# A front in a fixed order: loads on two queues, squares of x ahead of those of memory, x's products in place

## The chip, the cores and the metric

The kernel runs on one core of a Trainium2 chip. Its engines work side by side, each through its own queue in order: TensorE (PE, matrix products, with its weight loads listed as PEld), VectorE (DVE), ScalarE (ACT), GpSimd (POOL) and SyncE (SP, which here only issues DMAs). DMAs can be issued by SP, ACT and POOL. The metric is the device time of one execution in microseconds.

## The reference

One layer of a hybrid encoder over 512 frames of 1024 channels in float32, with 256 memory tokens:

```python
u = rmsnorm(h, g_mix[l])
proj = u @ w_in[l]
(gq, gk, gv, gg, ga, fq, fk, fv, ff, mq, gates) = split_cols(proj, PROJ_SIZES)
...
mkv = rmsnorm(mem, g_mem[l]) @ w_mem_kv[l]
mk, mv = jnp.split(mkv, 2, axis=-1)
...
merged = gt[:, :, 0] * y_gla + gt[:, :, 1] * y_fox + gt[:, :, 2] * y_mem
h = h + merged @ w_out[l]
u2 = rmsnorm(h, g_ffn[l])
h = h + jnp.square(jax.nn.relu(u2 @ w_ff1[l])) @ w_ff2[l]
```

Here `rmsnorm(x, g)` is `x * rsqrt(mean(x * x) + 1e-6) * g` over the channels. Three branches (gated linear attention, forgetting attention "FoX", cross attention to the memory) are merged, and an MLP and a last RMSNorm follow. The change touches only the start: the two norms, and the products of the normed memory and the normed x with the first weights.

## The kernel before

**Precision.** Each product of two float32 matrices is made as three products of fp32r parts. A matrix is split into hi (a cast to fp32r on ACT) and lo (the subtract raw - hi on DVE); `mm3` (L149) issues hi x hi, lo x hi and hi x lo into one PSUM tile. So every weight chunk of 128 x 1024 costs a DMA, a cast on ACT and a subtract on DVE, and the same holds for u, the normed x.

**Chunks.** `chunk_list` puts the weights in the order of use. Chunks 0 to 3 are the four key heads of the memory (`w_mem_kv`), 4 to 7 its values, 8 is "G" (low-rank and forget columns, split into the tile `both`), 9 is fq, 10 is fk (the first FoX pair), and 11 to 14 are fv. `load_w`, `split_w` and `get_w` (L132 to L147) load and split a chunk. Raw, hi and lo tiles have three buffers each, so a load waits until an earlier chunk has been split. `gT` and `gN` are generators that issue the products of one chunk or of four; one `next` is one step of three products (a `yield` each).

**The order.** PE runs in the order of the program (`manual_schedule`). On ACT, DVE, POOL and SP a scheduler writes the order ahead of time from its own estimate of the times: of what is ready it takes what was traced first, so later work can fill a gap. `tc.issue_after(ins)` puts what is traced in its block, on the engine of `ins`, behind `ins`.

**The front (L267 to L374).** Twelve products of zeros run first on PE while the first data are loaded. All loads are issued by SP: the columns, then mem (`memr`) in four quarters that alternate with four quarters of chunk 0, then chunk 1, constants, chunk 2, and x (`xr`, with channels on the partitions) in four quarters between chunks 3 and 4. Then:

- mem times `g_mem` is cast to `mxh` on ACT and its rest `mxl` is made on DVE (L301, L302). The norm's factor is applied later, to the products.
- `sq_cols` (L204) squares column block k on ACT and adds it to an accumulator. All sums of mem run on POOL; of x, blocks 1 to 3 on POOL and the others on DVE, in two accumulators.
- `mk_proj(h)` (L336) makes the keys of head h of the memory on PE, evacuates them on ACT, and squares two blocks of x.
- `rms_cols` (L216) sums an accumulator over the partitions by products with a column of ones; `rsqrt` makes the factor on DVE and POOL; `bcast_rows` (L232) spreads it over the partitions: one diagonal on ACT and one product on PE for each 128 frames, then a copy on ACT, to `rmb` (mem) and `rxb` (x).
- `mv` makes the memory's values, 16 steps, evacuated with mem's factor (L344).
- The loop of L359 makes u block by block: product x * `g_mix` * `rxb` on DVE into one of three scratch tiles `sg` (L371), cast to `uhi` on ACT, rest to `ulo` on DVE (L201, L202). For blocks 2 and 5 ACT scales x by `g_mix` beforehand and POOL makes the product (L369). Chunks G and fq are split at block 3.

**Behind it.** `low_rank` (L400) and fq go through PE block by block, five products for each block of u. `mem_split` (L376) scales and splits the memory's keys and values; it stands under `issue_after(u_end)`, where `u_end` is the last `ulo` on DVE. Then come fk (`run(pair)`), `decay_logs` (L418, whose first product is L421) and the four chunks of fv.

Of the kernel before, what the change touches and what calls it, by code (L numbers as in the profile page):

```python
# [3 lines left out]

# [57 lines left out]
def hybrid_block(ctx, tc, chunks, wst, xT, memT, xN, cols, gffn, gfin, wup, cst, out):  # L62
# [25 lines left out]
    def f(ap):  # L88
        return ap.bitcast(F32)
# [107 lines left out]
    def of(hi, lo):  # L197
        return lambda k, sl: (hi[:, k, sl], lo[:, k, sl])
# [2 lines left out]
        nc.scalar.copy(hi, src)  # L201
        return nc.vector.tensor_tensor(lo, src, f(hi), op=ALU.subtract).ins  # L202

    def sq_cols(pool_, src, n, k, accs, pool_ks, tag):  # L204

        e = 1 if k in pool_ks else 0
        eng = nc.gpsimd if e else nc.vector
        if accs[e] is None:
            accs[e] = dct[:, e * S:e * S + S] if n == S else pool_.tile([P, n], F32, tag=f"{tag}_acc{e}", name=nm("acc"))
            nc.scalar.activation(accs[e], src[:, k, :], AF.Square)  # L210
        else:
            sq = pool_.tile([P, n], F32, tag=f"{tag}_sq{e}", name=nm("sq"), bufs=2)
            nc.scalar.activation(sq, src[:, k, :], AF.Square)
            eng.tensor_tensor(accs[e], accs[e], sq, op=ALU.add)

    def rms_cols(pool_, accs, n):  # L216

        accs = [a for a in accs if a is not None]
        ps = at_()
        for t in range(n // P):  # L220
            for i, a in enumerate(accs):
                nc.tensor.matmul(ps[:, t:t + 1], a[:, t * P:(t + 1) * P], ones[:, 0:1], start=i == 0, stop=i == len(accs) - 1)
        return rsqrt(pool_, ps[:, :n // P], 1.0 / D, n // P)

    def rsqrt(pool_, ss, inv, n):
# [6 lines left out]
    def bcast_rows(pool_, r, n, rb):  # L232

        ps = at_()
        for t in range(n // P):
            dg = pool_.tile([P, P], F32, tag="dg", name=nm("dg"), bufs=4)
            nc.scalar.mul(dg, ident, r[:, t:t + 1])
            nc.tensor.matmul(ps[:, t * P:(t + 1) * P], ones, dg, start=True, stop=True)
        nc.scalar.copy(rb, ps[:, :n])
# [27 lines left out]
    with pool("front") as fp:  # L267
        rmb = la[:, 0, :]
        rxb = sg[3]
        memr = fp.tile([P, KT, M], F32, name="memr")  # L270
        xr = fp.tile([P, KT, S], F32, name="xr")
        pre = {}

        def lead(key, n, i):
            if key not in pre:
                late = index[key] > 2
                pre[key] = [(fp if late else wp).tile([P, 1024], F32, tag="lead" if late else "raw", name=nm("raw"),
                                                      bufs=2 if late else 3)]
                pre[key] += [wp.tile([P, 1024], F32R, tag=g, name=nm(g)) for g in ("hi", "lo")]
            sl = slice(i * 1024 // n, (i + 1) * 1024 // n)  # L280
            raw, hi, lo = (t[:, sl] for t in pre[key])
            nc.sync.dma_start(raw, wst[index[key]][:, sl])
            nc.scalar.copy(hi, raw)
            nc.vector.tensor_tensor(lo, raw, f(hi), op=ALU.subtract)
# [10 lines left out]
        nc.scalar.activation(warm, warm, AF.Exp)  # L295
        nc.sync.dma_start(cols_s, cols)
        macc, xacc = [None, None], [None, None]
        for j in range(4):
            nc.sync.dma_start(memr[:, 2 * j:2 * j + 2], memT[:, 2 * j:2 * j + 2])
            for k in (2 * j, 2 * j + 1):  # L300
                nc.scalar.mul(mxh[:, k, :], memr[:, k, :], gmem[:, k:k + 1])  # L301
                nc.vector.scalar_tensor_tensor(mxl[:, k, :], memr[:, k, :], gmem[:, k:k + 1], f(mxh[:, k, :]),  # L302
                                               op0=ALU.mult, op1=ALU.subtract)
                if k == 2 * j:
                    lead(chunks[0], 4, j)
        lead(chunks[1], 1, 0)
        nc.sync.dma_start(cst_s[:, :2 * P], cst[:, :2 * P])
        nc.sync.dma_start(cst_s[:, 5 * P:], cst[:, 5 * P:])
        lead(chunks[2], 1, 0)
        for j in range(4):  # L310
            nc.sync.dma_start(xr[:, 2 * j:2 * j + 2], xT[:, 2 * j:2 * j + 2])
            if j == 1:
                lead(chunks[3], 1, 0)
        lead(chunks[4], 1, 0)
        nc.sync.dma_start(cst_s[:, 2 * P:5 * P], cst[:, 2 * P:5 * P])
        nc.sync.dma_start(wup_s, wup)
        for k in range(KT):
            sq_cols(fp, memr, M, k, macc, range(KT), "m")

        get_plain = get_w  # L320

        def get_first(key):
            return pre[key][1:] if key in pre else get_plain(key)

        get_w = get_first
        UP = (2, 5)

        def mk_evac(h):
            raw = mk_raw(h)
            nc.vector.tensor_tensor(raw, raw, rmb, op=ALU.mult)  # L330
            split(mkh[:, h, :], mkl[:, h, :], raw)

        def mk_raw(h):
            return gkT[h // 2][:, (h % 2) * M:(h % 2) * M + M]

        def mk_proj(h):  # L336
            run(gT(("T", "w_mem_kv", P * h), mxh, mxl, lambda ps: nc.scalar.copy(mk_raw(h), ps[:, :M]), n=M))
            for k in (2 * h, 2 * h + 1):
                sq_cols(fp, xr, S, k, xacc, (1, 2, 3), "x")
                if k in UP:  # L340
                    nc.scalar.mul(xr[:, k, :], xr[:, k, :], gmix[:, k:k + 1])
# [4 lines left out]
        mk_proj(0)
        mk_proj(1)
        rm = rms_cols(fp, macc, M)
        mk_proj(2)
        bcast_rows(fp, rm, M, rmb)  # L350
        mk_proj(3)
        rx = rms_cols(fp, xacc, S)
        nc.vector.tensor_copy(msk_s, cst_s[:, 5 * P:5 * P + 64])
        mv = gN([("N", "w_mem_kv", 2 * j, 512) for j in range(4)], of(mxh, mxl), 2, mmt, mv_evac)
        for _ in range(4):
            next(mv)
        bcast_rows(fp, rx, S, rxb)
        run(islice(mv, 9))
        for k in range(KT):  # L359
            if k == 3:  # L360
                raw = load_w(("G",))
                raw3, w3 = (t.rearrange("p (k c) -> p k c", k=KT) for t in (raw, both))
                nc.scalar.copy(both, raw)
                low = slice(64, P)
                nc.vector.tensor_tensor(w3[:, :, low], raw3[:, :, low], f(w3[:, :, low]), op=ALU.subtract)
                first_q = get_w(("T", "w_in", OFF["fq"]))
            ut = sg[k % 3]
            if k in UP:
                nc.gpsimd.tensor_tensor(ut, xr[:, k, :], rxb, op=ALU.mult)  # L369
            else:  # L370
                nc.vector.scalar_tensor_tensor(ut, xr[:, k, :], gmix[:, k:k + 1], rxb, op0=ALU.mult, op1=ALU.mult)  # L371
            u_end = split(uhi[:, k, :], ulo[:, k, :], ut)
        run(mv)
# [23 lines left out]
    with pool("fox") as xp:  # L397
# [162 lines left out]
        pair = fox_pair(0)  # L560
        for _ in low_rank():
            next(pair)
        with tc.issue_after(u_end):
            mem_split()
        run(pair)
        decay_logs()
        fv = v_chunks(OFF["fv"], v_evac)
        run(islice(fv, 14))
        decay_sums()
# [855 lines left out]
```

## Time and profile before

| what | value |
|---|---|
| median of 3 runs | 816.14 us (815.4 to 816.98) |
| the profiled execution's own time | 815.97 us |
| its span | 814.2 us |
| granted PE clock over the span | 0.994 of full |
| DMA, whole program | 160.75 MB, mean 197 GB/s |
| to 55.5 us: busy PE / DVE / ACT / POOL | 49.50 / 39.30 / 39.38 / 17.35 us |

The profile is one execution. A row of the timeline has a start and a duration in us, engine, line, operation, output and inputs by the program's names, the shape, a count, and in brackets the engine's idle time before it and what ended that. The span of a PE product contains the time in which it passes through the array, so successive products overlap: their price is the distance of the starts. Issue rows of DMAs (SPq, ACTq, POOLq) show the issuing, not the transfer. A window's row has its bounds, its length, the busy time of PE, PEld, DVE, ACT and POOL with the number of instructions, the granted clock, the share of time the DMA engines worked, and GB/s.

### The profile page before, as it was taken

To read this page: it belongs to the slowest core of one execution; us is meant where nothing else is said; L and a number is where in the kernel's file an instruction comes from. 1 tells how busy PE (TensorE), PEld (TensorE's weight loads), DVE (VectorE), ACT (ScalarE), POOL (GpSimd) and SP (SyncE) were. 2 spreads that over 40 slices of the span, in tenths; PEclk is the share of its full clock that TensorE was granted. 3 is DMA by queue.
4 is the path that set the end of the run, shared out by engine and by line. 5 is a ranking of instruction groups with operands and counts; after the bars stand their busy time and mean duration, and the time that the engine had idled before them with its cause. 6 is when DMAs were issued, how large, how long until landed. Compare 5 with 4: busy or idle time off the path is not lost.

```text
span 814.2 us, 12094 instructions
## 1 busy us (share of the span) xinstructions
PE 797.0 (98%) x4625; PEld 681.2 (84%) x4625; DVE 575.6 (71%) x875; ACT 458.2 (56%) x726; POOL 117.5 (14%) x134
## 2 busy tenths in 40 slices
PE   7999999999999999999999999999999999999994
PEld 5878887778888888888888889988998899889983
DVE  5772654454565488585969658885788678878886
ACT  8763554443554346464645546764676377547764
POOL 5201322000000033111110000011001000100131
PEclk9999999999999999999999999999999999999998
DMA  8534968777858768789873706889658956895684
GB/s 313 204 104 138 284 206 225 214 226 208 260 156 224 242 180 183 184 207 234 213 187 113 279 7 225 224 197 221 212 167 196 260 186 164 192 262 186 146 140 129
DMA packets 41034, 160.75 MB, mean 197 GB/s; under 512 B 4952, under 2 KB 6032, under 8 KB 38928
## 3 DMA queue, kind: packets, MB, share of 16 engines
q0 software_dynamic: 11488, 60.30, 35.9%
q1 hardware_dynamic: 27648, 94.93, 33.4%
q10 hardware_dynamic: 1840, 4.75, 1.7%
q8 instruction: 36, 0.59, 0.3%
q14 instruction: 22, 0.18, 0.1%
HBM read 156.26 MB, written 31.49 MB: 231 GB/s over the span
## 4 chain that ended last, share of the span: by engine, by line
PE 93%; DVE 2%; ACT 1%; issue 1%; DMA 1%; POOL 1%; SPq 0%; ACTq 0%; DVEq 0%; POOLq 0%
PE mm L150 20%; PE mm L152 20%; PE mm L151 20%; PE a L150 4%; PE a L151 4%; PE a L152 4%; PE mm L923 3%; PE mm L924 3%; PE mm L925 3%; PE a L924 2%; PE a L923 2%; PE a L925 2%; PE a L547 1%; DMA raw<-in_wst_dram 1%; PE a L503 1%
## 5 line engine op out<-in xcount | busy, mean ns | idle before, releaser
L201 ACT CAST hi<-raw 128x1024 fp32r<-128x1024 f32 x77 | 80.8, 1050 | 62.8 <-PE mm L151 34.3
L202 DVE TENSOR_TENSOR lo<-raw,hi 128x1024 fp32r<-128x1024 f32 x77 | 94.1, 1222 | 30.4 <-ACT hi L201 30.4
L142 DVE TENSOR_TENSOR wlo<-raw,whi 128x1024 fp32r<-128x1024 f32 x49 | 63.0, 1288 | 67.2 <-ACT whi L141 58.7
L141 ACT CAST whi<-raw 128x1024 fp32r<-128x1024 f32 x49 | 51.5, 1052 | 90.6 <-issue 31.5
L1232 POOL DMA_DIRECT2D Y<-in_wst_dram x32 | 27.3, 854 | 263.0 <-DVE lo L202 194.5
L201 ACT CAST hi<-Y 128x1024 fp32r<-128x1024 f32 x40 | 41.9, 1048 | 39.8 <-PE mm L152 29.3
L152 PE MATMUL mm<-u2h,lo 128*128 128x256 f32 x224 | 63.4, 283 | 0.0
L151 PE MATMUL mm<-u2l,hi 128*128 128x256 f32 x224 | 63.4, 283 | 0.0
L150 PE MATMUL mm<-u2h,hi 128*128 128x256 f32 x224 | 63.4, 283 | 0.0
L202 DVE TENSOR_TENSOR lo<-Y,hi 128x1024 fp32r<-128x1024 f32 x40 | 48.9, 1222 | 19.7 <-ACT hi L201 19.6
L151 PE MATMUL mm<-lo,ch 128*128 128x512 f32 x160 | 62.3, 389 | 0.0
L150 PE MATMUL mm<-hi,ch 128*128 128x512 f32 x160 | 62.3, 389 | 0.0
L152 PE MATMUL mm<-hi,cl 128*128 128x512 f32 x160 | 62.2, 389 | 0.0
L150 PE MATMUL mm<-uhi,whi 128*128 128x512 f32 x128 | 50.7, 396 | 0.0
L152 PE MATMUL mm<-uhi,wlo 128*128 128x512 f32 x128 | 49.9, 390 | 0.0
L151 PE MATMUL mm<-ulo,whi 128*128 128x512 f32 x128 | 49.8, 389 | 0.0
L201 ACT CAST hi<-g 128x1024 fp32r<-128x1024 f32 x30 | 31.6, 1054 | 30.4 <-PE a L925 12.3
L202 DVE TENSOR_TENSOR lo<-g,hi 128x1024 fp32r<-128x1024 f32 x30 | 36.6, 1220 | 16.7 <-ACT hi L201 16.6
L150 PE MATMUL mm<-u2sh,hi 128*128 128x256 f32 x168 | 47.5, 283 | 0.0
L151 PE MATMUL mm<-u2sl,hi 128*128 128x256 f32 x168 | 47.5, 283 | 0.0
L152 PE MATMUL mm<-u2sh,lo 128*128 128x256 f32 x168 | 47.5, 283 | 0.0
L151 PEld LDWEIGHTS mm<-u2l,hi 128*128 128x128 f32 x224 | 43.0, 192 | 0.2
(415 smaller groups left out, 2261.0 us busy)
## 6 DMA issues: line engine op xcount, KB each, us to landing
raw<-in_wst_dram SPq DMA_DIRECT2D x109, 512.0 KB, 5.3
Y<-in_wst_dram POOLq DMA_DIRECT2D x32, 512.0 KB, 5.5
raw<-T SPq DMA_DIRECT2D x28, 512.0 KB, 3.4
T<-in_wst_dram POOLq DMA_DIRECT2D x12, 1024.0 KB, 8.9
g<-in_wst_dram POOLq DMA_DIRECT2D x24, 512.0 KB, 5.8
Y<-in_wst_dram SPq DMA_DIRECT2D x16, 512.0 KB, 4.4
g<-in_wst_dram SPq DMA_DIRECT2D x12, 512.0 KB, 3.2
nFb<-dF ACTq DMA_DIRECT2D x8, 448.0 KB, 11.0
```

What stands on the lines that cost most here:

```text
L141: cast = nc.scalar.copy(hi, raw)
L142: nc.vector.tensor_tensor(lo, raw, f(hi), op=ALU.subtract)
L150: nc.tensor.matmul(ps, lh, rh, start=start, stop=False)
L151: nc.tensor.matmul(ps, lh, rl, start=False, stop=False)
L152: nc.tensor.matmul(ps, ll, rh, start=False, stop=stop)
L201: nc.scalar.copy(hi, src)
L202: return nc.vector.tensor_tensor(lo, src, f(hi), op=ALU.subtract).ins
L503: nc.tensor.matmul(pss[e][:, :w], q[half[e], sl], k[half[e], :w], start=a == 0, stop=a == 2)
L923: nc.tensor.matmul(ps[t], a, wh[:, kk, :], start=go, stop=False, **w)
L924: nc.tensor.matmul(ps[t], a, wl[:, kk, :], start=False, stop=False, **w)
L925: nc.tensor.matmul(ps[t], b, wh[:, kk, :], start=False, stop=k == 3, **w)
L1232: nc.gpsimd.dma_start(to, x, accum_op=ALU.add)
```

## The change

The front is rewritten. The new `in_order` chains all ACT, DVE and PE instructions traced in its block: each gets an edge (issue order only) to the one traced before it on the same engine.

- ACT issues the columns and the four quarters of chunk 0, and SP issues mem, then chunk 1, a quarter of x, chunk 2, a quarter, chunk 3, two quarters, two constants, chunk 4. The other constants and `wup` follow behind the squares of mem.
- mem's products and the split of chunk 0 run first, then the splits of chunks 1 and 2, then the keys with the squares of x between the heads. `rms_cols` of x stands in the middle of head 3.
- Squares of mem come later: three ahead of the values, five behind the broadcast of x's factor. All sums are made on DVE, with one accumulator each for x and mem.
- `rms_cols` of mem and its broadcast stand at blocks 0 and 2 of the loop over u.
- x's products are made in place in `xr`, all on DVE; POOL makes none, and ACT no longer scales blocks 2 and 5.
- `mem_split`, fk and `decay_logs` all stand under `issue_after` of the last cast and of the last `ulo`. The mask's copy to `msk_s` moves there.

```diff
+    def in_order():
+        traced = nc.cur_bb.bb.instructions
+        n, mark = len(traced), traced[-1]
+        yield
+        start = next(k for k in reversed(range(len(traced))) if traced[k] is mark) + 1
+        ends = {}
+        for i in traced[start:]:
+            if i.engine in (nc.scalar.engine, nc.vector.engine, nc.tensor.engine):
+                if i.engine in ends:
+                    tc.add_manual_dep(i, ends[i.engine].name,
+                                      mybir.DependencyInfo(mybir.DependencyClass.NoSync, mybir.DependencyReason.DATA),
+                                      reason="in_order")
+                ends[i.engine] = i
+
+    def sq_col(pool_, src, n, k, acc, tag):
+        if k == 0:
+            nc.scalar.activation(acc, src[:, 0, :], AF.Square)
...
+            nc.scalar.activation(sq, src[:, k, :], AF.Square)
+            nc.vector.tensor_tensor(acc, acc, sq, op=ALU.add)
...
+        def first_load(i, n=1):
...
+                (nc.scalar if n > 1 else nc.sync).dma_start(raws[i][:, sl], wst[index[FIRST_W[i]]][:, sl])
...
+        def first_split(i, n=1, j=0):
...
+            cast = nc.scalar.copy(ready[i][0][:, sl], raws[i][:, sl])
+            nc.vector.tensor_tensor(ready[i][1][:, sl], raws[i][:, sl], f(ready[i][0][:, sl]), op=ALU.subtract)
...
+        def first_w(i):
+            run(first_load(i))
+            first_split(i)
...
+        with in_order():
+            nc.scalar.dma_start(cols_s, cols)
+            quarters = first_load(0, 4)
+            for j in range(4):
+                nc.sync.dma_start(memr[:, 2 * j:2 * j + 2], memT[:, 2 * j:2 * j + 2])
+                next(quarters)
+            nc.scalar.activation(warm, warm, AF.Exp)
+            run(first_load(1))
+            nc.sync.dma_start(xr[:, 0:2], xT[:, 0:2])
+            run(first_load(2))
...
+            for k in range(KT):
+                nc.scalar.mul(mxh[:, k, :], memr[:, k, :], gmem[:, k:k + 1])
+                nc.vector.scalar_tensor_tensor(mxl[:, k, :], memr[:, k, :], gmem[:, k:k + 1], f(mxh[:, k, :]),
+                                               op0=ALU.mult, op1=ALU.subtract)
+                if k % 2 == 0:
+                    first_split(0, 4, k // 2)
+            first_split(1)
+            first_split(2)
+            run(mk_proj(0))
+            x_squares(0, 1, 2, 3)
+            first_split(3)
+            run(mk_proj(1))
+            x_squares(4, 5)
+            run(mk_proj(2))
+            x_squares(6, 7)
+            first_split(4)
+            mk3 = mk_proj(3)
+            run(islice(mk3, 4))
+            rx = rms_cols(fp, xacc, S)
+            run(mk3)
+            first_w(5)
+            for k in range(3):
+                sq_col(fp, memr, M, k, macc, "m")
+            mv = gN([("N", "w_mem_kv", 2 * j, 512) for j in range(4)], of(mxh, mxl), 2, mmt, mv_evac)
+            run(islice(mv, 5))
+            bcast_rows(fp, rx, S, rxb)
+            for k in range(3, KT):
+                sq_col(fp, memr, M, k, macc, "m")
+            nc.sync.dma_start(cst_s[:, 2 * P:5 * P], cst[:, 2 * P:5 * P])
+            nc.sync.dma_start(wup_s, wup)
+            for k in range(KT):
+                if k == 0:
+                    first_w(6)
+                    run(islice(mv, 4))
+                    rm = rms_cols(fp, macc, M)
+                if k == 2:
+                    first_w(7)
+                    bcast_rows(fp, rm, M, rmb)
+                    run(islice(mv, 4))
+                if k == 3:
...
+                    nc.scalar.copy(both, raw)
+                    low = slice(64, P)
+                    nc.vector.tensor_tensor(w3[:, :, low], raw3[:, :, low], f(w3[:, :, low]), op=ALU.subtract)
+                    first_w(9)
+                    first_q = ready[9]
+                ut = xr[:, k, :]
+                nc.vector.scalar_tensor_tensor(ut, ut, gmix[:, k:k + 1], rxb, op0=ALU.mult, op1=ALU.mult)
+                cast = nc.scalar.copy(uhi[:, k, :], ut)
+                u_end = nc.vector.tensor_tensor(ulo[:, k, :], ut, f(uhi[:, k, :]), op=ALU.subtract)
+            run(mv)
+        u_ends = cast.ins, u_end.ins
...
-        with tc.issue_after(u_end):
+        with tc.issue_after(u_ends[0]), tc.issue_after(u_ends[1]):
             mem_split()
-        run(pair)
-        decay_logs()
+            run(pair)
+            nc.vector.tensor_copy(msk_s, cst_s[:, 5 * P:5 * P + 64])
+            decay_logs()
```

More of the change, by code (lines that the diff above doesn't have):

```diff
@@ L1 @@
-from contextlib import ExitStack
+from contextlib import ExitStack, contextmanager
 from functools import partial
@@ L202, in split, with rms_cols @@
         return nc.vector.tensor_tensor(lo, src, f(hi), op=ALU.subtract).ins
[L204 to L210, printed above, removed]
+    @contextmanager
+    def in_order():
[14 more added lines that the diff above has]
+            nc.scalar.activation(acc, src[:, 0, :], AF.Square)
         else:
-            sq = pool_.tile([P, n], F32, tag=f"{tag}_sq{e}", name=nm("sq"), bufs=2)
+            sq = pool_.tile([P, n], F32, tag=f"{tag}_sq", name=nm("sq"), bufs=3)
             nc.scalar.activation(sq, src[:, k, :], AF.Square)
-            eng.tensor_tensor(accs[e], accs[e], sq, op=ALU.add)
-    def rms_cols(pool_, accs, n):
-        accs = [a for a in accs if a is not None]
+            nc.vector.tensor_tensor(acc, acc, sq, op=ALU.add)
+    def rms_cols(pool_, acc, n):
         ps = at_()
         for t in range(n // P):
-            for i, a in enumerate(accs):
-                nc.tensor.matmul(ps[:, t:t + 1], a[:, t * P:(t + 1) * P], ones[:, 0:1], start=i == 0, stop=i == len(accs) - 1)
+            nc.tensor.matmul(ps[:, t:t + 1], acc[:, t * P:(t + 1) * P], ones[:, 0:1], start=True, stop=True)
         return rsqrt(pool_, ps[:, :n // P], 1.0 / D, n // P)
@@ L271, in hybrid_block, with get_first @@
         xr = fp.tile([P, KT, S], F32, name="xr")
[L272 to L284, printed above, removed]
+        FIRST_W = [chunks[j] for j in range(8)] + [("G",), ("T", "w_in", OFF["fq"])]
+        raws, ready = {}, {}
+        def first_load(i, n=1):
+            late = i in (3, 4)
+            raws[i] = (fp if late else wp).tile([P, 1024], F32, tag="lead" if late else "raw", name=nm("raw"),
+                                                bufs=2 if late else 3)
+            for j in range(n):
+                sl = slice(j * 1024 // n, (j + 1) * 1024 // n)
+                (nc.scalar if n > 1 else nc.sync).dma_start(raws[i][:, sl], wst[index[FIRST_W[i]]][:, sl])
+                if n > 1:
+                    yield
+        def first_split(i, n=1, j=0):
+            if i not in ready:
+                ready[i] = [wp.tile([P, 1024], F32R, tag=g, name=nm(g)) for g in ("hi", "lo")]
+            sl = slice(j * 1024 // n, (j + 1) * 1024 // n)
+            cast = nc.scalar.copy(ready[i][0][:, sl], raws[i][:, sl])
+            nc.vector.tensor_tensor(ready[i][1][:, sl], raws[i][:, sl], f(ready[i][0][:, sl]), op=ALU.subtract)
+            if i > 4:
+                next_sum(cast.ins)
+        def first_w(i):
+            run(first_load(i))
+            first_split(i)
+        get_plain = get_w
+        def get_first(key):
+            return ready[FIRST_W.index(key)]
+        get_w = get_first
         mxh = fp.tile([P, KT, M], F32R, name="mxh")
         mxl = fp.tile([P, KT, M], F32R, name="mxl")
+        macc = fp.tile([P, M], F32, name="macc")
+        xacc = dct[:, :S]
         warm = fp.tile([P, 1], F32, name="warm")
@@ L294, in hybrid_block, with mk_raw @@
             nc.tensor.matmul(ps, wz[:, :P], wz, start=True, stop=True)
[L295 to L326, printed above, removed]
+        def mk_raw(h):
+            return gkT[h // 2][:, (h % 2) * M:(h % 2) * M + M]
         def mk_evac(h):
@@ L331, in mk_evac @@
             split(mkh[:, h, :], mkl[:, h, :], raw)
-        def mk_raw(h):
-            return gkT[h // 2][:, (h % 2) * M:(h % 2) * M + M]
         def mk_proj(h):
[L337 to L341, printed above, removed]
+            return gT(("T", "w_mem_kv", P * h), mxh, mxl, lambda ps: nc.scalar.copy(mk_raw(h), ps[:, :M]), n=M)
@@ L343, in mv_evac @@
         def mv_evac(t, ps):
             nc.scalar.mul(gqT[t], ps, rm[:, t:t + 1])
[L346 to L372, printed above, removed]
@@ L373, in hybrid_block, with x_squares @@
-        run(mv)
+        def x_squares(*ks):
+            for k in ks:
+                sq_col(fp, xr, S, k, xacc, "x")
+        with in_order():
[8 more added lines that the diff above has]
+            run(first_load(2))
+            nc.sync.dma_start(xr[:, 2:4], xT[:, 2:4])
+            run(first_load(3))
+            for j in range(2, 4):
+                nc.sync.dma_start(xr[:, 2 * j:2 * j + 2], xT[:, 2 * j:2 * j + 2])
+            nc.sync.dma_start(cst_s[:, :2 * P], cst[:, :2 * P])
+            nc.sync.dma_start(cst_s[:, 5 * P:], cst[:, 5 * P:])
+            run(first_load(4))
+            for k in range(KT):
[38 more added lines that the diff above has]
+                if k == 3:
+                    raw = load_w(("G",))
+                    raw3, w3 = (t.rearrange("p (k c) -> p k c", k=KT) for t in (raw, both))
+                    nc.scalar.copy(both, raw)
[8 more added lines that the diff above has]
+            run(mv)
```

## The prediction

> **What bounds the kernel now.** I read the page's header and engine shares first, then what PE (TensorE) waited for, then the windows that part the start from the rest, and only then the timelines of each engine up to 56 us.
>
> ```profile
> span 814.2 us, 12094 instructions
> PE 797.0 (98%) x4625; PEld 681.2 (84%) x4625; DVE 575.6 (71%) x875; ACT 458.2 (56%) x726; POOL 117.5 (14%) x134
> ```
> ```profile
> PE mm L152 <- DVE lo L284: 2.2, 5, 0.8
> PE mm L404 <- DVE ulo L202: 1.5, 1, 1.5
> ```
> ```profile
> 55.50:814.20 758.70, 747.52 (x4374) 641.86 (x4373) 536.32 (x818) 418.83 (x652) 100.18 (x116) 1.00 0.72 196
> ```
>
> PE is busy for 98% of the span. The list of PE's waits (us in total, times, longest) has its largest entries in the front. From 55.5 us on PE works for 747.5 of 758.7 us, and the missing 11 are mostly the output's tail. So the time is PE's dense run behind the front: a front that ends x us later ends the kernel x us later. As milestone I take the first product of L421 (decay_logs), which PE reaches after the mem projections, the low-rank product and the first fq and fk:
>
> ```profile
> 55.56 1.95 PE L421 MATMUL a<-wup_s,dct 128*128 128x264 f32 x8
> ```
>
> Rows that start ahead of it show what the front loses and what its steps cost:
>
> ```profile
> 6.28 0.38 PE L150 MATMUL mm<-mxh,hi 128*128 128x256 f32 x1
> ...
> 23.88 1.95 PE L222 MATMUL a<-cst_s,dct 128*128 128x1 f32 x16 [0.27 <-DVE dct L214]
> ...
> 26.81 0.63 PE L150 MATMUL mm<-hi,mxh 128*128 128x512 f32 x1
> 27.24 0.63 PE L151 MATMUL mm<-lo,mxh 128*128 128x512 f32 x1
> ...
> 30.11 1.05 PE L238 MATMUL a<-dg,cst_s 128*128 128x128 f32 x8
> ...
> 39.21 0.39 PE L403 MATMUL mm<-uhi,both 128*128 128x512 f32 x1
> 39.44 0.39 PE L404 MATMUL mm<-ulo,both 128*128 128x512 f32 x1
> ...
> 43.77 0.40 PE L403 MATMUL mm<-uhi,both 128*128 128x512 f32 x1
> 45.68 0.50 PE L404 MATMUL mm<-ulo,both 128*128 128x512 f32 x1 [1.51 <-DVE ulo L202]
> ...
> 50.12 0.39 PE L150 MATMUL mm<-uhi,whi 128*128 128x512 f32 x1
> ```
>
> Read start to start: a 512-wide product takes 0.23 us (39.21 to 39.44), but 0.43 us at 26.8 to 27.2, just behind the 1.95 us of one-column products of rms_cols. About nine products run so, 1.8 us lost. The granted clock says the same:
>
> ```profile
> 27.00:28.00 1.00, 1.00 (x4) 0.80 (x3) 0.51 (x1) 0.00 (x0) 1.00 (x1) 0.50 0.62 143
> ```
>
> **The change part by part.** Edges now hold ACT, DVE and PE to the traced order, so I follow each queue by hand with durations of this trace.
>
> *Start and loads.* ACT issues five DMAs ahead of its table load. The issues cost SP 0.43 us each; the nearest rows of ACT's own:
>
> ```profile
> 2.59 0.43 SPq L282 DMA_DIRECT2D raw<-in_wst_dram  x1
> ```
> ```profile
> 70.19 4.82 ACTq L452 DMA_DIRECT2D dF<-dct  x7
> ```
> ```profile
> 0.73 1.28 ACT L295 ACT_TABLE_LOAD   x1 [0.73 <-PEq L1408]
> ...
> 4.41 0.91 ACT L301 ACTIVATE mxh<-memr,cols_s 128x256 fp32r<-128x256 f32 x2 [2.18 <-DMA memr<-in_memT_dram]
> ```
>
> Five issues are 2.2 us by SP's price, 3.4 by ACT's (4.82/7). With 1.28 and 0.2 behind, ACT is ready at 4.5 to 5.7. Now it starts at 4.41, held by a DMA. I take 4.5, and nothing at either end: ACT has slack ahead of its second and third chunk. The two queues shorten the issue, but the DMA engines are the limit soon:
>
> ```profile
> 4.00:5.00 1.00, 1.00 (x4) 0.31 (x3) 0.04 (x1) 0.59 (x2) 0.00 (x0) 1.00 0.92 287
> 15.00:16.00 1.00, 1.00 (x11) 1.00 (x10) 0.25 (x1) 1.00 (x3) 0.92 (x2) 1.00 1.03 410
> ```
>
> They are 92% busy at 4 us, so I give the loads 0.5 to 0.8 us, no more. Chunk 1 landed at 11.1; I put it at 10.2. Behind it 512 KB come every 1.28 us (410 GB/s): x's first quarter at 11.5, chunk 2, now behind that quarter, at 12.8. Both ends: 1.5 us either way, which shifts everything below by as much. [...]
>
> *Squares and sums.* mem's squares leave the early ACT stream, and their sums leave POOL. ACT's first stage is 8 x 0.455 (mxh) + 4 x 0.33 (casts of chunk 0) = 5.0 us, then chunk 1's cast. From chunk 2's landing ACT is a plain queue: two casts 1.9, three evacuations 0.8, eight squares 4.6, so to 20.1; DVE's last x sum ends at 21.2. The durations are these:
>
> ```profile
> 11.10 1.05 ACT L283 CAST hi<-raw 128x1024 fp32r<-128x1024 f32 x1 [0.31 <-DMA raw<-in_wst_dram]
> ...
> 15.52 1.14 ACT L213 ACTIVATE sq<-xr 128x512 f32<-128x512 f32 x2
> 17.18 0.35 ACT L337 COPY gkT<-mm 128x256 f32<-128x256 f32 x1
> ...
> 28.43 1.28 ACT L237 ACTIVATE dg<-cst_s,rr 128x128 f32<-128x128 f32 x4 [2.21 <-POOL rr L229]
> ...
> 32.22 0.57 ACT L239 COPY sg<-a 128x512 f32<-128x512 f32 x1
> ```
>
> One accumulator halves rms_cols of x, 1.95 to 0.95, and it moves into the middle of mk_proj(3): PE 21.2 to 22.2, the other half of that projection to 23.6. ACT waits there for the evacuation (23.8), then casts chunk 5 (0.95), squares mem three times (1.0) and makes four diagonals (1.3). PE fills this with 15 products and the broadcast (0.8), and rxb is copied at 28.2, against 32.2 now. So the first half gains **4.0 us**.
>
> *From rxb to the first product of x.* Now DVE goes on at 33.13, half a microsecond behind. In the new order there stand ahead of it: on ACT the copy 0.5, five mem squares 1.65, chunk 6's cast 1.05; on DVE its subtract 1.23; on PE two products that need it and rms_cols of mem, 1.3 with the way out; on DVE the ms. That is 28.2 + 5.9 = 34.1. The gain is gone, and 1.0 us more.
>
> *x's products.* Three scratch tiles let DVE run ahead; in place and in order it can't.
>
> ```profile
> 33.13 2.44 DVE L371 SCALAR_TENSOR_TENSOR sg<-xr,cols_s,sg 128x512 f32<-128x512 f32 x2
> ...
> 38.44 1.78 DVE L371 SCALAR_TENSOR_TENSOR sg<-xr,cols_s,sg 128x512 f32<-128x512 f32 x1
> 40.14 1.21 DVE L142 TENSOR_TENSOR wlo<-raw,whi 128x1024 fp32r<-128x1024 f32 x1
> ...
> 46.15 0.74 DVE L371 SCALAR_TENSOR_TENSOR sg<-xr,cols_s,sg 128x512 f32<-128x512 f32 x1
> 47.57 0.69 DVE L202 TENSOR_TENSOR ulo<-sg,uhi 128x512 fp32r<-128x512 f32 x1 [0.69 <-ACT uhi L201]
> 48.18 1.42 DVE L330 TENSOR_TENSOR gkT<-gkT,la 128x256 f32<-128x256 f32 x4
> 49.52 1.29 DVE L202 TENSOR_TENSOR mvl<-gqT,mvh 128x512 fp32r<-128x512 f32 x2
> 50.73 1.43 DVE L202 TENSOR_TENSOR mkl<-gkT,mkh 128x256 fp32r<-128x256 f32 x4
> ```
>
> The last step shows what each of the eight will be: product 46.15, cast on ACT, subtract 47.57, next DVE work 48.18: 2.03 us, with DVE idle in the middle and the next product queued behind the subtract. Eight are 16.2. Between them come chunk 7's subtract (0.35 wait + 1.14), G's and fq's (0.95 + 0.35 + 1.14, with waits on two casts): 3.9. POOL's two products go, and with them what their neighbours lost (1.22 and 1.78 instead of 0.74, some 2 us); that is already in the 2.03. ulo ends at 34.1 + 16.2 + 3.9 + 0.1 = 54.4, against 48.2 now. PE meanwhile waits 2.7 us for chunk 6 and 5.0 us for mem's diagonals, which stand on ACT behind the second cast of x; its own work would then end at 53.3, so the chain of x decides. fq ends at 55.5, against 50.1: **+5.4 us**.
>
> *fk behind the products.* In before, fk's split runs within the loop of x's products, its cast at 36.73 and its subtract at 40.14:
>
> ```profile
> 36.73 1.06 ACT L141 CAST whi<-raw 128x1024 fp32r<-128x1024 f32 x1
> ```
>
> The change traces it under issue_after. It may then issue only behind the last cast and subtract of x, and mem_split, traced earlier, stands ahead of it: on ACT two evacuations 1.2, the low-rank one 0.6, mkh 1.3, mvh 1.0, Q 0.5; on DVE 1.42 + 1.43 + 1.2 + 0.6. The cast ends at 59.5, the subtract at 60.8. PE, free at 55.5 (fq's end; fk began at 50.12 in before), gets its first fk product at 59.6, its second at 60.8, and 23 at 0.2275 us end at 66.1: **+5.1 us**. The lower end, fk first, is 0.7 us of wait; the upper, with later chunks' splits in between and their buffers taken first, 1.5 us more.
>
> *The clock.* After 2.4 us of next to no work the products slowed (above); after 1.51 us, at 45.68, they didn't. The waits of 5.0 and 4.1 us are longer. The first restart falls into slack; the second is 0 or 1.8 us. I take 0.9. Ends 0 and 3.6. [...]
>
> Late constants, wup and the mask's copy cost nothing: PE's work on mv covers them; without that cover the copy is 0.25 us.
>
> Sum: 5.4 + 5.1 + 0.9 = 11.4 us. The profiled execution took 815.97 us (1.8 beyond its span; the median is 816.14): 815.97 + 11.4 = **827.4 us**.
>
> **The rivals.** *fk is not held up*: the scheduler, which writes the order behind the fixed part, puts fk's split ahead of mem_split. For it: PE waits for nothing else. Against it: now mem_split went first at 48.18. Time: 816 + 5.4 + 0.7 + 0.4 = 822.5.
>
> *Faster*: the products of x overlap after all, because the edges leave DVE free to take the next product while ACT casts. Then PE alone sets the end: 28.0 + 33 products of mv 7.5, rms and broadcast 0.9, 40 products 9.1, fk 5.5 = 51.0, 4.5 us early, 811.5. This decides as soon as a step of x costs DVE less than 1.14 us of PE's five products beside it and mem's squares stay off the way. For it: rxb is 4 us sooner, and the slow clock at 26 us may go. Against it: the edges name every ACT and DVE instruction.
>
> *No change*: the order isn't binding where it hurts, or the 4 us are just spent by the late start of the products: 815 to 817.
>
> *Worse*: loads 1.5 us late and two cold restarts on the path: 831.
>
> **How the numbers follow.** The forecast with its own range of 825 to 831 has 0.5, fk early 0.22, something between these (819 to 825 or above 831) 0.11, faster 0.12, no change 0.05. Faster and no change are left out, and the low end lies below the fk rival by loads 1.5 us early and more overlap: 819 to 831. About 0.2% is what a measurement can tell from no change: slower 0.83, same 0.05, faster 0.12.
>
> **What would show it.** In DVE's timeline, product and subtract of x alternate with 0.7 us idle before each subtract and a step is 2.0 us; rxb's copy stands near 28 us, the first product near 34; PE waits about 5 us before the broadcast of mem, and about 4 us before fk, for an ACT cast. L421 stands at 66 to 67. The forecast is wrong if DVE shows two products in a row, if fk's cast comes before mkh's, or if the whole lateness isn't found again in the span.

## The result and the profile after

The change made the kernel slower: 824.45 us (median of 5 runs, 822.64 to 824.93) against 816.14 (815.4 to 817.59, 5 runs), a ratio of 1.0096 [1.0085, 1.0108]. The profiled execution took 824.93 us, 8.96 more than that of before; its span is 8.9 longer and its mean granted clock 0.989 (before 0.994). Of after's five executions one took 822.64 us at a mean granted clock of 0.991, the others 824.3 to 824.9 at 0.989; each profile is of one execution, up to 2.5 us off its kernel's median below.

The page of the kernel after, header and engine shares:

```profile
span 823.1 us, 12078 instructions
PE 799.7 (97%) x4617; PEld 681.8 (83%) x4617; DVE 577.2 (70%) x887; ACT 456.4 (55%) x724; POOL 102.5 (12%) x123
```

The list of PE's waits in after (total us, times, longest). The five waits for chunks and the one for x's last block, the longest entries of before, have given way to one long one:

```profile
PE a L247 <- ACT dg L246: 4.8, 1, 4.8
PE mm L150 <- ACT hi L298: 2.0, 2, 1.3
PE a L231 <- DVE dct L226: 1.5, 1, 1.5
```

The milestone, decay_logs' first product, is L460 now. PE's timeline and the window behind it:

```profile
64.33 1.95 PE L460 MATMUL a<-wup_s,dct 128*128 128x264 f32 x8
```
```profile
64.30:823.10 758.80, 747.63 (x4374) 641.84 (x4372) 535.71 (x819) 418.85 (x652) 99.63 (x116) 0.99 0.72 197
```

The milestone is 8.77 us late, and the stretch behind it is 758.8 us long as before (758.7) with the same busy time of PE (747.6 and 747.5). So the loss lies wholly in the front and passes to the end one for one. Where in the front, the timelines of the three engines tell. DVE, the loop over x:

```profile
36.19 0.74 DVE L408 SCALAR_TENSOR_TENSOR xr<-xr,cols_s,sg 128x512 f32<-128x512 f32 x1
37.62 0.69 DVE L410 TENSOR_TENSOR ulo<-xr,uhi 128x512 fp32r<-128x512 f32 x1 [0.68 <-ACT uhi L409]
38.23 0.74 DVE L408 SCALAR_TENSOR_TENSOR xr<-xr,cols_s,sg 128x512 f32<-128x512 f32 x1
...
55.82 0.69 DVE L410 TENSOR_TENSOR ulo<-xr,uhi 128x512 fp32r<-128x512 f32 x1 [0.69 <-ACT uhi L409]
56.43 1.43 DVE L330 TENSOR_TENSOR gkT<-gkT,la 128x256 f32<-128x256 f32 x4
```

Product, 0.68 us of idle time while ACT casts, subtract, next product: 36.19 to 38.23 is 2.04 us a step, and the whole loop, with three splits of chunks in it, takes 20.24 us (36.19 to 56.43). ACT in after, the start, x's broadcast and the end of the loop:

```profile
1.19 3.74 ACTq L290 DMA_DIRECT2D raw<-in_wst_dram  x4
...
6.36 0.49 ACT L361 ACTIVATE mxh<-memr,cols_s 128x256 fp32r<-128x256 f32 x1
...
12.94 1.05 ACT L298 CAST hi<-raw 128x1024 fp32r<-128x1024 f32 x1 [1.13 <-DMA raw<-in_wst_dram]
...
25.20 0.37 ACT L334 COPY gkT<-mm 128x256 f32<-128x256 f32 x1 [3.91 <-PE mm L152]
...
30.33 0.59 ACT L248 COPY sg<-a 128x512 f32<-128x512 f32 x1 [1.71 <-PE a L247]
...
55.69 1.26 ACT L337 ACTIVATE gqT<-mm,rr 128x512 f32<-128x512 f32 x2
56.84 1.99 ACT L141 CAST whi<-raw 128x1024 fp32r<-128x1024 f32 x2
58.73 0.62 ACT L201 CAST mvh<-gqT 128x512 fp32r<-128x512 f32 x1
```

The last three rows are where the prediction failed: behind the loop ACT evacuates, and then casts fk's weights and the next chunk's (whi, x2) *before* mvh. PE's timeline in after:

```profile
21.82 1.05 PE L231 MATMUL a<-cst_s,dct 128*128 128x1 f32 x8 [1.48 <-DVE dct L226]
...
23.17 0.28 PE L150 MATMUL mm<-mxh,hi 128*128 128x256 f32 x1
23.29 0.38 PE L151 MATMUL mm<-mxl,hi 128*128 128x256 f32 x1
...
24.11 0.41 PE L152 MATMUL mm<-mxh,lo 128*128 128x256 f32 x1
24.32 0.41 PE L150 MATMUL mm<-mxh,hi 128*128 128x256 f32 x1
...
33.66 0.50 PE L150 MATMUL mm<-hi,mxh 128*128 128x512 f32 x1 [1.28 <-ACT hi L298]
35.00 0.50 PE L151 MATMUL mm<-lo,mxh 128*128 128x512 f32 x1 [0.84 <-DVE lo L299]
...
57.37 0.39 PE L152 MATMUL mm<-uhi,lo 128*128 128x512 f32 x1
57.94 0.50 PE L150 MATMUL mm<-uhi,whi 128*128 128x512 f32 x1 [0.18 <-ACT whi L141]
58.28 0.40 PE L151 MATMUL mm<-ulo,whi 128*128 128x512 f32 x1
59.20 0.50 PE L152 MATMUL mm<-uhi,wlo 128*128 128x512 f32 x1 [0.53 <-DVE wlo L142]
```

fk's first product waits 0.18 us and its third 0.53. And half-width products are 0.12 us apart at 23.17 and 0.21 at 24.11: the clock has fallen, in a place that the prediction didn't name. The windows of after:

```profile
23.00:24.00 1.00, 1.00 (x8) 1.00 (x8) 0.07 (x1) 0.00 (x0) 0.85 (x1) 0.67 0.27 94
24.00:25.00 1.00, 1.00 (x7) 1.00 (x7) 0.00 (x0) 0.00 (x0) 0.17 (x1) 0.50 0.02 8
...
26.00:27.00 1.00, 1.00 (x5) 0.76 (x4) 0.45 (x1) 1.00 (x3) 0.00 (x0) 0.63 0.02 8
...
36.00:37.00 1.00, 0.08 (x1) 0.00 (x0) 0.82 (x2) 0.03 (x1) 0.65 (x1) 0.99 0.89 287
...
43.00:44.00 1.00, 1.00 (x4) 0.77 (x4) 0.69 (x1) 1.00 (x3) 0.00 (x0) 0.59 0.77 229
```

The granted clock is 0.50 from about 23.3 on (0.67 is a third of a window at full and two thirds at half); from 26.7 products are at full rate again, and from 37.0 to 43.8, around the wait for mem's broadcast, it is 0.50 once more. Eight half-width products lose 0.09 us each, and four full-width ones, 0.43 us apart instead of 0.23, 0.2 each: some 1.5 us in all, ahead of x's broadcast.

### The profile page after: what moved, and what is told of

Same layout as the page of the kernel before. It is cut to its first block, busy times and chain, and to the rows that moved or that the text cites. A ratio compares the mean times of both kernels' runs of the same rounds, so it can differ in the third digit from the quotient of the medians.

```text
span 823.1 us, 12078 instructions
## 1 busy us (share of the span) xinstructions
PE 799.7 (97%) x4617; PEld 681.8 (83%) x4617; DVE 577.2 (70%) x887; ACT 456.4 (55%) x724; POOL 102.5 (12%) x123
## 4 chain that ended last, share of the span: by engine, by line
PE 91%; DVE 3%; ACT 2%; DMA 1%; issue 1%; POOL 0%; ACTq 0%; SPq 0%; DVEq 0%
PE mm L150 20%; PE mm L152 19%; PE mm L151 19%; PE a L150 4%; PE a L152 4%; PE a L151 4%; PE mm L965 3%; PE mm L963 3%; PE mm L964 3%; PE a L963 2%; PE a L965 2%; PE a L964 2%; DMA raw<-in_wst_dram 1%; PE a L586 1%; PE a L542 1%
## 5 line engine op out<-in xcount | busy, mean ns | idle before, releaser
L142 DVE TENSOR_TENSOR wlo<-raw,whi 128x1024 fp32r<-128x1024 f32 x45 | 57.2, 1275 | 63.5 <-ACT whi L141 55.0
L141 ACT CAST whi<-raw 128x1024 fp32r<-128x1024 f32 x45 | 47.2, 1052 | 87.6 <-issue 31.5
L150 PE MATMUL mm<-uhi,whi 128*128 128x512 f32 x120 | 47.7, 398 | 0.2 <-ACT whi L141 0.2
L152 PE MATMUL mm<-uhi,wlo 128*128 128x512 f32 x120 | 46.9, 391 | 0.5 <-DVE wlo L142 0.5
L151 PE MATMUL mm<-ulo,whi 128*128 128x512 f32 x120 | 46.7, 389 | 0.0
```

Source lines behind the costliest of these rows:

```text
L141: cast = nc.scalar.copy(hi, raw)
L150: nc.tensor.matmul(ps, lh, rh, start=start, stop=False)
L151: nc.tensor.matmul(ps, lh, rl, start=False, stop=False)
L152: nc.tensor.matmul(ps, ll, rh, start=False, stop=stop)
```

## The experiments

Each kernel ran beside before on the same chip (before's medians there: 816.16, 816.23 and 816.26 us). Ratios are to before; the milestone is the start of decay_logs' first product in the profiled execution, so small differences between milestones can be those between executions.

| kernel | what differs | median us | ratio [95%] | milestone us |
|---|---|---|---|---|
| after | | 824.45 | 1.0096 [1.0085, 1.0108] | 64.3 |
| x1_fk_free | fk out of the hold | 823.54 | 1.0083 [1.0068, 1.0098] | 63.2 |
| x2_pipe | product k+1 ahead of subtract k | 820.67 | 1.0049 [1.0031, 1.0067] | 60.8 |
| x3_early | squares and splits into ACT's wait | 819.21 | 1.0034 [1.0023, 1.0044] | 58.2 |
| x4_early_pipe | x2 and x3 | 814.43 | 0.9978 [0.9965, 0.9992] | 53.7 |
| x5_free | no fixed order | 827.84 | 1.0139 [1.0118, 1.0159] | 65.4 |
| x10_free_early | x5 with x3's regrouping | 815.38 | 0.9985 [0.9974, 0.9996] | 53.5 |
| x6_zeros | zero products ahead of rms_cols | 822.93 | 1.0079 [1.0062, 1.0095] | 62.6 |
| x7_sp | after, all early loads on SP | 825.12 | 1.0112 [1.0093, 1.0131] | 65.4 |
| b1_queues | before, two queues | 817.09 | 1.0010 [1.0000, 1.0020] | 56.5 |
| b2_dve | before, x's products all on DVE | 815.46 | 0.9981 [0.9969, 0.9993] | 52.5 |
| x8_best | x4, x1, x6, mem's broadcast behind x's | 813.96 | 0.9970 [0.9959, 0.9981] | 53.3 |
| x9_next | x8, chunk 2 ahead of x's first quarter | 814.32 | 0.9975 [0.9966, 0.9984] | 53.9 |

**fk and the hold (x1_fk_free).** From after, fk leaves the block under issue_after:

```diff
             mem_split()
-            run(pair)
+        run(pair)
+        with tc.issue_after(u_ends[0]), tc.issue_after(u_ends[1]):
             nc.vector.tensor_copy(msk_s, cst_s[:, 5 * P:5 * P + 64])
             decay_logs()
```

> The changed kernel with fk taken out of the block behind x's last product (only mem_split, the mask's copy and decay_logs stay in it). Theory A, from the trace after: fk costs PE only about 1.0 us there (waits of 0.18 and 0.53 us and the restart between them), and its subtract, free to move, goes into the gap of DVE's alternation of product and subtract and lengthens it by about 0.4 us for each such split: 824.0 to 825.0 us, no gain. Theory B, the step of the prediction (fk held back is worth 5.1 us): 819 to 820 us.

The median fell by 0.9 us, with intervals that overlap: half a microsecond below A's range, which gave it nothing, and B's four to five us are refuted. The timelines of x1_fk_free, DVE and PE, show why:

```profile
45.59 0.74 DVE L408 SCALAR_TENSOR_TENSOR xr<-xr,cols_s,sg 128x512 f32<-128x512 f32 x1
46.25 1.22 DVE L142 TENSOR_TENSOR wlo<-raw,whi 128x1024 fp32r<-128x1024 f32 x1
47.39 0.68 DVE L410 TENSOR_TENSOR ulo<-xr,uhi 128x512 fp32r<-128x512 f32 x1
47.99 0.74 DVE L408 SCALAR_TENSOR_TENSOR xr<-xr,cols_s,sg 128x512 f32<-128x512 f32 x1
```
```profile
57.74 0.39 PE L150 MATMUL mm<-uhi,whi 128*128 128x512 f32 x1
```

fk's wait is gone (57.74, no bracket, and 5.45 us from there to the milestone, as in before). But its subtract, and fv's first, now take 1.22 us in the 0.7 us gaps of x's chain, so that two of its steps take 2.4 us. The loop ends 0.13 us later than in after, although rms_cols ran 0.62 us sooner in this execution (21.20). So the hold costs 1.3 us at fk and saves about 0.75 in the loop.

**The chain of x's products (x2_pipe).** DVE's order is turned: product k+1 stands ahead of subtract k, so that ACT casts meanwhile.

```diff
+                for j in ((0, 1) if k == 0 else (k + 1,) if k + 1 < KT else ()):
+                    nc.vector.scalar_tensor_tensor(xr[:, j, :], xr[:, j, :], gmix[:, j:j + 1], rxb, op0=ALU.mult, op1=ALU.mult)
                 ut = xr[:, k, :]
-                nc.vector.scalar_tensor_tensor(ut, ut, gmix[:, k:k + 1], rxb, op0=ALU.mult, op1=ALU.mult)
```

> The changed kernel with x's product of block k+1 traced ahead of the subtract of block k, nothing else. Theory A (product, cast and subtract one after the other set the end, 20.2 us from 36.2 to 56.4): the loop takes about 14 to 15 us, but PE, which waits for mem's diagonals until about 40, then has 21 products of mv and 40 of the low-rank and fq ones, so fq ends near 55.0 in place of 57.6, and fk's split is done by then: 820.5 to 821.5 us. Theory B (only the late start of the products counts): 824 to 825. Theory C (the loop is the only chain, PE follows at once): 818.5.

820.67 us, 3.8 less than after and inside A's range. No work was taken away, only the order of DVE's instructions was changed, so that order cost those 3.8 us. Not all of them lie in the loop: fk's delay of 1.3 us is gone too, since PE goes from fq to fk without a wait. More wasn't to be had by this alone. What PE waits for is chunk 6 and mem's broadcast, and behind the broadcast it works without a break up to the milestone, until 43.2 us at a granted clock of 0.50. PE in x2_pipe:

```profile
38.93 1.23 PE L247 MATMUL a<-dg,cst_s 128*128 128x128 f32 x4 [3.48 <-ACT dg L246]
```

**What stands between the broadcast and the loop (x3_early).** ACT in after is idle for 3.9 us ahead of 25.20, until PE has finished the keys' last head. Chunk 5's cast and all squares of mem go there, chunk 6 follows, and rms_cols of mem comes ahead of x's broadcast:

```diff
-            run(mk3)
             first_w(5)
-            for k in range(3):
+            for k in range(KT):
                 sq_col(fp, memr, M, k, macc, "m")
+            run(mk3)
+            first_w(6)
...
-            run(islice(mv, 5))
+            run(islice(mv, 4))
+            rm = rms_cols(fp, macc, M)
+            run(islice(mv, 1))
             bcast_rows(fp, rx, S, rxb)
-            for k in range(3, KT):
-                sq_col(fp, memr, M, k, macc, "m")
...
-                    first_w(6)
                     run(islice(mv, 4))
-                    rm = rms_cols(fp, macc, M)
```

> The changed kernel with chunk 5's split and all eight squares of mem traced ahead of the last half of head 3, where ACT waits 3.9 us for PE, chunk 6's split right behind it, and mem's rms_cols ahead of the broadcast of x's factor. Theory A (5.9 us of other work stand between rxb's copy and the first product): the first product starts near 31 in place of 36.2, the loop stays 20.2 us, fq ends near 52.3: 819 to 820 us. Theory B (the loop's end is set by something else, or the moved work delays rxb by as much): 822 to 824.5.

819.21 us, 5.2 less than after, as A has it. Five squares, a cast and a subtract no longer stand between rxb's copy (29.46) and the first product of x, and the clock stayed at 1.00 from 20 to 30 us in its profile. DVE in x3_early:

```profile
30.08 0.75 DVE L407 SCALAR_TENSOR_TENSOR xr<-xr,cols_s,sg 128x512 f32<-128x512 f32 x1 [1.61 <-ACT sg L248]
```

In the two profiles this product comes 6.1 us sooner than in after. The shorter stretch behind rxb gives 5.2, the clock 1.5 and an earlier rms_cols 0.7; the work moved ahead of rxb takes 1.3 back. So the regrouping itself is worth some 4 us there, and a part of the 5.2 us between the medians may be the clock's.

**Both (x4_early_pipe).**

> Both of the two edits before. Theory A: the loop runs from about 31 to 45 to 46, and PE sets the end: mem's diagonals near 35.5, then 21 and 40 products, fq's end near 50.5, fk ready: 816.5 to 817.5 us, about the kernel before. Theory B, the two gains simply add (3.4 and 5.0): 815.5 to 816.3. Theory C, the scheduled order behind the front is worse too: above 818.

814.43 us: 10 us less than after, below before, and faster than any of the three theories. The profile of x4_early_pipe: DVE in the loop, then PE's waits, then a window.

```profile
39.86 0.75 DVE L407 SCALAR_TENSOR_TENSOR xr<-xr,cols_s,sg 128x512 f32<-128x512 f32 x1
40.52 0.68 DVE L410 TENSOR_TENSOR ulo<-xr,uhi 128x512 fp32r<-128x512 f32 x1
41.13 0.74 DVE L407 SCALAR_TENSOR_TENSOR xr<-xr,cols_s,sg 128x512 f32<-128x512 f32 x1
```
```profile
PE a L231 <- DVE dct L226: 1.3, 1, 1.3
PE a L247 <- ACT dg L246: 1.3, 1, 1.3
```
```profile
24.00:25.00 1.00, 1.00 (x6) 0.82 (x6) 0.79 (x3) 0.60 (x2) 0.80 (x1) 1.00 0.19 45
```

A step of x takes 1.27 us, with no bracket: DVE is never idle. Mem's broadcast is waited for 1.3 us, where after waits 4.8, x2 3.5 and x3 2.6. And the granted clock is 1.00 in every window from 21 to 46 us, though PE waits 1.3 us ahead of x's rms_cols here too. Theories A and B were 1 to 3 us too long. The shorter wait and the full clock both go that way; how the difference divides between them wasn't measured.

**The clock (x6_zeros).** Six full-width products of zeros, which nothing reads, stand in PE's wait ahead of x's rms_cols:

```diff
+            ps = at_()
+            for _ in range(6):
+                nc.tensor.matmul(ps, wz[:, :P], wz, start=True, stop=True)
             rx = rms_cols(fp, xacc, S)
```

> The changed kernel with six products of zeros on PE in its wait ahead of rms_cols of x (1.48 us). Theory A (the granted clock falls to 0.50 at 23.4 because PE had next to nothing to do from 20.2 to 22.7, and costs 1.6 us that pass on to rxb and to the end): the clock stays at 1.00 from 22 to 28, 822.6 to 823.4 us. Theory B (the narrow products alone let it fall, or what decides lies behind): 824.2 to 825.

822.93 us (822.54 to 823.02), 1.5 less than after, in A's range; the milestone is 1.7 us sooner. The windows of x6_zeros:

```profile
24.00:25.00 1.00, 1.00 (x7) 0.82 (x7) 0.00 (x0) 0.73 (x2) 0.00 (x0) 1.00 0.01 4
...
40.00:41.00 1.00, 1.00 (x4) 0.87 (x4) 0.74 (x2) 0.56 (x2) 0.00 (x0) 0.50 0.00 0
```

At 24 us the clock is full. This one window wouldn't prove that the zeros did it, since in x3 the clock stays up there without them; the times of the four executions speak for it. Behind the 4.85 us wait for mem's broadcast the clock is 0.50, as in after. In after that costs nothing, because PE still waits for x's last subtract (0.23 us). In x6 the low clock lasts until 44.5 us and PE goes from the broadcast to fq's end without a wait; fq's end lies 2.04 us behind the start of the last subtract instead of 1.78, so it costs about 0.3.

**No fixed order (x5_free, x10_free_early).** The block of in_order becomes `if True:`, in x5 from after and in x10 from x3, so the scheduler may order ACT, DVE and POOL.

> The changed kernel without the chain of edges: the scheduler orders ACT and DVE by its own estimate, with the same trace. Theory A (the fixed order of DVE and ACT is what costs): mem's squares and the splits fill ACT's wait, x's eight products run one behind the other ahead of the subtracts, and the kernel is faster by 4 to 7 us: 817 to 820 us. Theory B (the loss lies in the loads, the single accumulator and DVE alone making sums and products): 823 to 825.

> The kernel of x5 (no chain of edges) with the regrouping of x3, so that mem's factor is made on POOL before DVE starts on x's products. Theory A (in x5 PE waited 10.5 us for mem's broadcast, because POOL's power, 0.7 to 1.1 us elsewhere, took 5.86 us beside DVE's run of subtracts and splits): the power takes 0.7 to 2 us, the wait goes, 814 to 817 us. Theory B (the scheduler's order is worse in itself): 822 or more.

x5 fits no theory: 827.84 us, slower than after. The products do overlap, as the "faster" theory wanted: x's last subtract ends at 43.1 us, 13 sooner than in after. But PE waits 10.5 us for mem's broadcast. The timelines of x5_free, of DVE, POOL, ACT and PE in turn:

```profile
37.60 0.15 DVE L237 TENSOR_SCALAR ms<-a 128x2 f32<-128x2 f32 x1
37.67 1.22 DVE L299 TENSOR_TENSOR lo<-raw,hi 128x1024 fp32r<-128x1024 f32 x1
38.80 4.29 DVE L410 TENSOR_TENSOR ulo<-xr,uhi 128x512 fp32r<-128x512 f32 x7
```
```profile
37.84 5.86 POOL L238 TENSOR_TENSOR rr<-ms,cst_s 128x2 f32<-128x2 f32 x1 [11.85 <-DVE ms L237]
```
```profile
43.73 0.69 ACT L246 ACTIVATE dg<-cst_s,rr 128x128 f32<-128x128 f32 x2 [6.00 <-POOL rr L238]
```
```profile
44.19 1.22 PE L247 MATMUL a<-dg,cst_s 128*128 128x128 f32 x4 [10.53 <-ACT dg L246]
```

The wait has two parts. PE had mem's sums ready at 33.65, but DVE took ms only behind all eight products of x, at 37.60. Then the power of mem's norm, two numbers for each partition, took 5.86 us on POOL, beside DVE's subtracts, and ended 0.6 us behind them. That the subtracts slowed it is an inference from their times. In x10 mem's squares come early, so that ms and the power run ahead of the loop. The timeline of x10_free_early, POOL:

```profile
30.43 0.71 POOL L238 TENSOR_TENSOR rr<-ms,cst_s 128x2 f32<-128x2 f32 x1 [4.46 <-DVE ms L237]
```

The same instruction takes 0.71 us, PE no longer waits for the broadcast, and the kernel takes 815.38 us, inside theory A's range; its profiled execution, with the milestone at 53.5, took 813.87. So neither the fixed order nor its absence decides: with the squares early both beat before, and the free order doesn't need x2's edit.

**The queues (x7_sp, b1_queues) and POOL's products (b2_dve).** x7 gives the columns and the quarters back to SP in after; b1 gives them to ACT in before; b2 sets `UP = ()` in before, so that all of x's products run on DVE.

> The changed kernel with the columns and chunk 0's quarters issued by SP again. Theory A (ACT's five issues hold its first cast until 6.4 in place of 4.4, but ACT then waits 1.1 us for chunk 2, landed at 12.9, so the late start is covered): first product on PE near 6.2, chunk 2 at 12.8 to 13.5, the same time within 0.6 us, 823.9 to 825. Theory B (the late start goes on to the end): 822 to 823. Theory C (two queues carry the loads faster): 825.5 or more.

> The kernel before with the columns and chunk 0's quarters issued by ACT, its order left to the scheduler. Theory A (ACT is 90 to 98% busy from 5 to 25 us in before, so 1 to 2 us of issuing push its casts and squares): 817 to 818 us. Theory B (the loads come sooner by the issue time saved): 815 to 815.8. Theory C (nothing): 816 to 816.5.

> The kernel before with all eight of x's products on DVE (POOL makes none, ACT scales no block), its order left to the scheduler. Theory A: POOL's two products cost their neighbours on DVE 2.0 us (1.22 and 1.78 in place of 0.74), and two more on DVE cost 1.3, so this part of the change is worth nothing to a small gain: 815.2 to 816.4 us. Theory B (DVE is the bound of this stage and the products on POOL carried it): 817 to 818.

x7 took 0.7 us more than after, between the ranges of A and C and with an interval that overlaps after's. ACT in x7_sp starts earlier, at 4.84 us, but then waits for loads:

```profile
13.97 1.05 ACT L298 CAST hi<-raw 128x1024 fp32r<-128x1024 f32 x1 [1.51 <-DMA raw<-in_wst_dram]
```

Chunk 2 is cast at 13.97 instead of 12.94: the two queues bring it 1 us sooner. In before they are worth nothing: b1 is 0.8 us slower, in A's range and at the edge of what can be measured, and whether for A's reason isn't shown. b2 gained 0.8 us, as expected: x's products all on DVE, a part of the change, are no loss by themselves. Its milestone overstates this: the profiled execution took 812.96 us, 2.5 less than its median, and its clock stayed at 1.00 from 23 to 29 us, where that of before fell.

**The best order (x8_best, x9_next).** x8 takes x4, x1 and x6 together and moves mem's broadcast right behind x's; x9 also loads chunk 2 ahead of x's first quarter and puts mem's broadcast at block 1.

> The two edits of x4 together with mem's broadcast right behind x's, fk free, and the six products of zeros. Theory A (with work for PE at every point the front is bound by PE): the broadcast of x ends near 29, 33 products of mv, 40 of the low-rank and fq ones follow without a wait, fq ends near 47, 3 us ahead of the kernel before: 812.5 to 814 us. Theory B (DVE's and ACT's chain of x still ends last): 815 to 817.

> As x8, with chunk 2 loaded ahead of x's first quarter and mem's broadcast one block later. Theory A (from chunk 2's landing to rms_cols of x DVE and ACT work without a break, so a landing 1.2 us sooner passes on, and the wait of 0.97 us before mem's broadcast goes): rms_cols of x near 20.2, L421's like at 51.3 to 52.3: 811.8 to 812.8 us. Theory B (x's first quarter, then later, holds the squares instead): 813.5 to 814.3.

x8 is the fastest kernel of the study, 813.96 us, in A's range and 2.3 below before (0.9970 [0.9959, 0.9981]). Against x4 the gain can't be told from none; PE still waits 1.0 us for mem's broadcast. x9 gains nothing more: its rms_cols of x came at 21.33 us, in x8 at 21.19, since DVE now waited 0.95 us for a square of x, whose first quarter lands later. That is B's reason, and its range was met within 0.02 us.

## Why the prediction was right, and where not

It said slower, 827.4 us in a range of 819 to 831; the median is 824.45. The stated range held, but the forecast's own band of 825 to 831 was missed by 0.55 us, and the median lies in the stretch that had a chance of 0.11. By its own steps, from the profiled execution:

| step | predicted | measured |
|---|---|---|
| chunk 2 | 12.8 us | cast at 12.94, waited for |
| rms_cols of x | 21.2 | 21.82 |
| copy of rxb | 28.2 | 30.33 |
| rxb to x's first product | 5.9 | 5.86 |
| loop over x | 20.2 | 20.24 |
| PE's wait for chunk 6 / mem's diagonals | 2.7 / 5.0 | 2.1 / 4.85 |
| end of fq against before | +5.4 | +7.5 (57.37 + 0.23) |
| fk's delay | +5.1 | +1.3 |
| clock | +0.9, at fk's restart | +1.5, behind rms_cols of x |
| milestone against before | +11.4 | +8.8 |

**Right** was the main mechanism: products in place and in a fixed order cost a full step of product, cast and subtract each, and what stands between broadcast and loop eats the gain of the earlier rms_cols. Both durations were met within 0.1 us. x2 and x3 each take one of the two away and win 3.8 and 5.2 us, fk's delay and the clock included; together they bring the kernel below before. That the lateness passes to the end one for one held in all kernels: milestone and span are 758.6 to 758.8 us apart in each.

**Wrong was the step "fk behind the products"**, 5.1 us. It took it that mem_split, traced earlier, stands ahead of fk's split on ACT and DVE. The scheduler put fk's cast right behind the evacuations, before mvh and mkh, and its subtract at 57.92. That is the order of the rival "fk is not held up", whose price of 0.7 us for the waits was met (0.18 + 0.53); with the wider distance behind each wait (0.34 us to the next product instead of 0.23) it is 1.3: from fq's end at 57.60 to the milestone are 6.73 us, against 5.44 in before (50.12 to 55.56). The prediction itself had named fk's cast ahead of mkh's as a sign that it is wrong, and the sign came. The rival's total, 822.5, was too low for another reason, the next one.

**Mis-sized was the clock**, and put in the wrong place. It was charged at fk, where the long wait didn't come, and forgotten behind rms_cols of x, where PE waits 1.48 us and then does 0.9 us of one-column products. The prediction had shown that before slows behind its one-column products, and still counted the new order's products there at the full rate. It costs 1.5 us on the path, and x6 wins as much back.

Whether such a stretch lowers the clock isn't decided by its length alone. In after the clock changes at 23.34, 26.74, 36.98 and 43.82 us by the windows above: 3.40, 10.24 and 6.84 us apart, which is once, three times and twice 3.41. In x1 it changes at 22.67, 26.09, about 36.3 and 43.15, by the starts of its products and its windows (0.83 from 20 to 30 us, 1.00 to 36, 0.66 to 46), so at about the same distances. The slow stretch of before, 26.04 to 29.45 (0.52 from 26 to 27 us, 0.50 to 29, 0.77 to 30), is 3.41 us long. Up to rms_cols of x, x1 and x3 give PE the same products; in both it waits 1.08 us there, and the one-column products are over at 22.1. In x1 the clock then fell, in x3 it stayed at 1.00 until about 34.3 (1.00 from 20 to 30 us, 0.86 to 36). What made the difference isn't shown by these profiles.

The remaining 0.6 us are the start: rms_cols of x at 21.82. The same code gave 21.2 in x1, x2 and x3 and 21.5 in x4, so most of that is scatter between executions. ACT was ready at 6.36, later than both bounds (4.5 to 5.7). The price of an issue was right: the four took 0.33 to 0.45 us each. But the row of 3.74 us holds a pause, as the fourth started at 4.6 only, and the row from which the upper bound was taken holds one too (seven issues, 0.32 us in the middle, 1.77 the longest). The wait of 1.13 us for chunk 2 covered the late start, as the prediction's slack had it.

The sum as it went: 0.6 (start) + 1.5 (clock) + 5.4 (x's chain) + 1.3 (fk) = 8.8 us, against 8.77 at the milestone and 8.96 in the profiled times. The prediction's 11.4 came within 2.6 of it partly by luck: fk was 3.8 us too dear, the start and the clock were 0.6 us too cheap each.

## What to carry to other kernels

In an order written by hand, an engine whose step waits for another engine's answer needs the next step's work ahead of that wait: product k+1 before subtract k turned steps of 2.04 us into 1.27 here. Before fixing an order, list each engine's idle stretches and move into them what else would stand in the chain; x3's regrouping did that and gave 5.2 us, of which the clock may be a part. What a scheduler will put first behind a hold can't be read from the order of tracing alone: price both orders, and take the chance of each from what is ready when the hold ends. Before two profiles are compared in tenths of a microsecond, look at where the clock fell in each: the lapse of before, 3.41 us at a granted clock of 0.50, is worth up to 1.7 us by estimate, half its length.

## What the runs showed of the hardware

- POOL beside DVE: the power of 128x2 numbers took 0.70 us in x3 with DVE idle, 1.14 in after beside one product of x, and 5.86 in x5 beside a subtract of 1.22 us and a run of seven. That of 128x4 took 1.02 us in after with DVE idle, and 1.94 in x3 beside a subtract and sums. None of these runs isolates what lengthened it; in x10 that of 128x2 took 0.71 us.
- DMA issue: on ACT a quarter of chunk 0 took at most 0.45 us to issue in after, on SP 0.43 in before. With two queues the first eight DMAs had left by 2.6 us, with SP alone by 4.4; but the ninth left at 4.43 in after and at 4.49 in before. The trace puts SP's pause in after (1.9 us) down to the landing of a quarter of mem; what sets it isn't shown.
- Clock: in after its changes in the front lie 3.40, 10.24 and 6.84 us apart, in x1 3.42, about 10.2 and 6.8, and before's slow stretch is 3.41 us long. After the same wait of 1.08 us and the same one-column products it fell in x1 and stayed up in x3.
